# A hybrid decoder layer: weight tiles of the MLP's chunk loop begin at other places, one transpose goes to another bank

## The chip, the core and the metric

The kernel runs on one NeuronCore of a Trainium2 chip. Its engines are TensorE (PE, matrix products into PSUM banks), VectorE (DVE), ScalarE (ACT), GpSimd (POOL) and SyncE (SP, which here only issues transfers). Each has its own queue of instructions and works through it in order; they wait for each other by semaphores. The metric is the device time of one execution in microseconds (us), lower is better.

## The reference

One decoder layer on 256 tokens of width 2048, in float32: a normalised input goes through one wide projection, half of it through sliding-window attention and half through a gated linear recurrence, both through an output projection, and the result is added to the input. Then comes the MLP, which is the part that matters here:

```python
h = rmsnorm(x, mlp_pre_gain[layer])
u = jax.nn.relu(jnp.einsum('bsd,df->bsf', h, w_up[layer]))
y = jnp.einsum('bsf,fd->bsd', u * u, w_down[layer])
x = x + rmsnorm(y, mlp_post_gain[layer])
```

`w_up` is 2048 x 8192 and `w_down` is 8192 x 2048.

## The kernel before

**Split weights.** Every weight tile (128 x 4 x 512 values, 1 MB) is loaded as float32, then split in two: ACT casts it to a rounded high tile `whi` (line 90), DVE subtracts that from the original and leaves the low tile `wlo` (line 91). PE multiplies high by high, high by low and low by high, so a product needs its high tile first and its low tile one matmul later.

**Chunk loop.** The MLP's inner width of 8192 is cut into 8 chunks of 1024. Chunk 0 is computed ahead of the loop with another set of tiles. From chunk 1 on, the up projection is done by Strassen's scheme: a chunk's weights are four quarters named X, P, Q (the lower right one) and R, with X loaded or added up several times (`X+P`, `X+Q` and so on, line 871, on DVE), and seven block products m1 to m7 in place of eight. In between stand the down projections of the chunk before (`d` tiles, lines 111 to 113, into bank `sc`). The loop is a list of segments; each uses one weight tile for 12 products (`up_seg`, line 867) or 24 (`down_seg`). For chunk 1 the list begins with the two halves of m1, the second half of chunk 0's first down column, the two halves of m5, then down, m6, down, m7.

**Order.** From line 657 on for PE and line 715 on for ACT, DVE and SP the order is that of the code (`manual_schedule`). For each segment k the loop at the end writes: the additions of segment k on DVE; the split of segment k + 2 (`prepare(k + 2)`: cast on ACT, subtraction on DVE); ACT's other work and the transposes ("turns") of segment k; its products; its loads. So a cast that waits holds up everything behind it on ACT.

**Rings.** Tiles of one tag share a ring of slots. A new tile takes a slot when the tile before in it is done with, and its first writer waits for that tile's last readers. At the loop's start the old pool of weight tiles (four slots for `whi`, four for `wlo`, three for raw tiles) is closed and the new one (`wpool_c`) is laid over the same memory, with two slots each for X, d, P and Q and three each for `whi` and `wlo`. What the first tiles of the new pool wait for is thus decided by which old tile lay there. Of the old tiles the last to be read is the pair `w00`, the first down tile of chunk 0, whose 24 products (`down_half(0, 0, 0, ...)`) are the last on PE before the loop. Before those come four blocks of up products with the old pairs 4, 5, 6 and 7, in this order.

In the built program of before, the first cast of the loop (X, segment 0) goes into the slot of the high tile of `w00`, the first Q tile into that of old high tile 5, the second Q tile into that of the low tile of `w00`, and the low tiles into the slots of old low tiles 7, 5 and 6. A tile named `unused` is asked for ahead of the first cast and never written.

**Turns.** A turn transposes a 128 x 512 tile on PE into a PSUM bank (four transposes), then ACT and DVE split it. Two turns bring sums of the activations (`turn_sum`, line 637, into banks `tr` and `o`, read by ACT line 639 and DVE line 640). Two more bring the second half of chunk 0's activations (`turn_u`, transposes line 669, square line 671 and cast 673 on ACT, subtraction 674 on DVE): the first into the third `sc` bank, the second into `tr`, which it shares with the first `turn_sum`. The turns' results `uT` are read by the first down segment of the loop.

Of the kernel before, what the change touches and what calls it, by code (L numbers as in the profile page):

```python
# [8 lines left out]
F32 = mybir.dt.float32  # L9
F32R = mybir.dt.float32r  # L10
# [5 lines left out]
P = 128  # L16
# [13 lines left out]
def tile_hybrid_layer(  # L30
# [17 lines left out]
    nc = tc.nc  # L48
# [13 lines left out]
    wp = [pool_w.__enter__()]  # L62
# [18 lines left out]
    def split_weight(src, raw=None, pieces=1, bufs=4, between=None):  # L81
        raw = load_raw(src) if raw is None else raw
        hi = wp[0].tile(list(raw.shape), F32R, tag="whi", name=nm("whi"), bufs=bufs)
        if between:
            between()
        lo = wp[0].tile(list(raw.shape), F32R, tag="wlo", name=nm("wlo"), bufs=bufs)
        n = raw.shape[1] // pieces
        for i in range(pieces):
            k = slice(i * n, (i + 1) * n)
            nc.scalar.copy(out=hi[:, k], in_=raw[:, k])  # L90
            nc.vector.tensor_tensor(out=lo[:, k], in0=raw[:, k], in1=hi[:, k].bitcast(F32), op=ALU.subtract)  # L91
        return hi, lo
# [573 lines left out]
    def turn_u(uT, cb, tb, u, tag, bufs):  # L666
        tp = bank(tag, bufs)
        for i in range(4):
            nc.tensor.transpose(tp[:, i * P:(i + 1) * P], u[:, i * P:(i + 1) * P], ident)
        u2 = upool.tile([P, 4, P], F32, tag="u2", name=nm("u2"), bufs=2)  # L670
        nc.scalar.activation(out=u2, in_=tp.rearrange("p (a t) -> p a t", a=4), func=AF.Square)
        hi, lo = (uT[cb][:, :, i, tb * P:(tb + 1) * P] for i in range(2))
        nc.scalar.copy(out=hi, in_=u2)
        nc.vector.tensor_tensor(out=lo, in0=u2, in1=hi.bitcast(F32), op=ALU.subtract)
# [120 lines left out]
    def half(tb, h):  # L795
        return hn[tb][:, h * 1024:(h + 1) * 1024]
# [4 lines left out]
    def turn_sum(src, c, tag="sc", bufs=3):  # L801
        t = sums[src[0]]
        turn_act(src[1][:, c * 512:(c + 1) * 512], *(t(slice(4 * c, 4 * c + 4), i) for i in range(2)), tag, bufs)
# [52 lines left out]
    def raw_tile(tag, wv, kt0, c0):  # L856
        t = wp[0].tile([P, 4, 512], F32, tag=tag, name=nm(tag), bufs=2)
        nc.sync.dma_start(out=t, in_=wv[:, kt0:kt0 + 4, c0:c0 + 512])
        return t
# [63 lines left out]
    def relu_first(tb):  # L923
        prev[1, tb] = new_u()
        relu(prev[1, tb], ps[tb])
# [15 lines left out]
    def load_up(name, ch, h):  # L941
        kt0 = (8 if name in "QR" else 0) + 4 * h
        raws[name, ch, h] = raw_tile("P" if name == "R" else name, w_up_v, kt0, ch * 1024 + (512 if name in "PQ" else 0))
# [44 lines left out]
    def t(ch, cb, tb, dst, tag="sc", bufs=3):  # L988
        return lambda: turn_u(uTs[dst], cb, tb, us[ch][cb, tb], tag, bufs)

    def period(ch, m1_next):
        d = ch - 1
# [7 lines left out]
        if ch == 1:  # L1000
            q = [None, m1_first[0], m1_first[1], dn[0][1], m5[0], m5[1], dn[1][0], m6[0], m6[1], dn[1][1],
                 m7[0], m7[1], dn[2][0], m3[0], m3[1], dn[2][1], m4[0], m4[1], m2[0], m2[1],
                 m1_next[0], dn[3][0], m1_next[1], dn[3][1]]
        else:
            q = [m5[0], m5[1], dn[0][0], m6[0], m6[1], dn[0][1], m7[0], m7[1], dn[1][0], m3[0], m3[1], dn[1][1],
                 m4[0], m4[1], dn[2][0], m2[0], m2[1], dn[2][1], m1_next[0], dn[3][0], m1_next[1], dn[3][1]]
# [34 lines left out]
        if ch == 1:  # L1041
            q[1].turns += [lambda c=c: turn_sum(("s4", half(0, 0)), c, ("tr", "o")[c], 1) for c in range(2)]
            q[1].turns.append(t(d, 1, 0, d))
            q[2].turns.append(t(d, 1, 1, d, "tr", 1))
            loads = [(1, "d", d, 1, 1), (4, "d", d, 2, 0), (7, "d", d, 2, 1),
                     (8, "R", ch, 0), (9, "R", ch, 1), (10, "d", d, 3, 0), (11, "Q", nx, 0), (12, "Q", nx, 1),
                     (13, "d", d, 3, 1), (14, "X", nx, 0), (15, "X", nx, 1), (16, "P", nx, 0), (17, "P", nx, 1),
                     (19, "d", ch, 0, 0), (21, "d", ch, 0, 1)]
        else:
            q[0].turns += [t(d, 0, 0, d), t(d, 0, 1, d)]  # L1050
            q[3].turns.append(t(d, 1, 0, d))
            q[4].turns.append(t(d, 1, 1, d))
            loads = [(0, "d", d, 1, 0), (3, "d", d, 1, 1), (5, "R", ch, 0), (6, "R", ch, 1), (6, "d", d, 2, 0),
                     (9, "d", d, 2, 1), (12, "d", d, 3, 0), (15, "d", d, 3, 1),
                     (17, "d", ch, 0, 0), (19, "d", ch, 0, 1)]
            if nx < NCH:
                loads += [(8, "Q", nx, 0), (9, "Q", nx, 1), (11, "X", nx, 0), (12, "X", nx, 1), (14, "P", nx, 0),
                          (15, "P", nx, 1)]
# [14 lines left out]
    for ch in range(1, NCH):  # L1073
        m1 = first_products(ch + 1) if ch < NCH - 1 else [None, None]
        part, q = period(ch, m1)
        if ch == 1:
            q[3].adds.append(late_y)
        if ch < NCH - 1:
            part[-1].loads.append(lambda ch=ch: uTs.update({ch: new_uT()}))
        else:  # L1080
            last = NCH - 1
            q[14].turns.append(lambda: uTs.update({last: new_uT("mu2", "mu3")}))
            q[14].turns.append(t(last, 1, 1, last, "pj"))
            q[15].turns.append(t(last, 1, 0, last, "pj"))
            q[16].turns.append(t(last, 0, 1, last, "pj"))
            q[19].turns.append(t(last, 0, 0, last, "pj"))

            def load_residual():
                tail["x2"] = []
                for tb in range(2):  # L1090
                    xr = wp[0].tile([P, D], F32, tag="X", name=nm("x2"), bufs=2)
                    nc.sync.dma_start(out=xr, in_=x2_dram[tb])
                    tail["x2"].append(xr)

            def load_gain():
                tail["g"] = wp[0].tile([P, D], F32, tag="Q", name="gmlp", bufs=2)
                nc.sync.dma_start(out=tail["g"], in_=mlp_post.broadcast_to([P, D]))

            q[21].loads.append(load_gain)
        segs += part  # L1100
# [17 lines left out]
    def prepare(k, between=None):  # L1118
        segs[k].w = split_weight(None, segs[k].raw(), bufs=3, between=between)

    wp[0].tile([P, 4, 512], F32R, tag="whi", name="unused", bufs=3)
    prepare(0, lambda: [load_up("Q", 1, h) for h in range(2)])
    relu_first(0)
    prepare(1)
    relu_first(1)
# [46 lines left out]
```

## Time and profile before

| | us |
|---|---|
| three runs | 1112.05, 1112.89, 1113.70; median 1112.89 |
| profiled execution, its time | 1112.53 |
| its span | 1110.8 |
| PE busy | 1084.3 (98%) |
| DVE busy | 816.2 (73%) |
| ACT busy | 622.8 (56%) |
| POOL busy | 37.6 (3%) |

The profile's times count from the span's start; 1.7 us of the execution lie outside the span. The chunk loop begins at 466 us. A matmul's end is modelled, and matmuls overlap in the pipeline, so on PE the starts are the times to go by: a 128 x 512 product starts every 0.227 us when nothing holds it. In an idle time "<-" names what ended it.

### The profile page before, as it was taken

What the parts mean: (1) busy time and instruction counts of PE and PEld (TensorE: products, weight loads), DVE (VectorE), ACT (ScalarE), POOL (GpSimd) and SP (SyncE); (2) the same over time, 40 slices, a digit from 0 to 9 for tenths busy, and PEclk for the clock granted to TensorE, in tenths of its full rate; (3) what the DMA queues carried; (4) which work ended last, traced back from release to release, by engine and by line L of the source; (5) the groups of instructions that cost most, each with busy time, mean ns of one, the idle gap of its engine ahead of it and who ended that gap; (6) DMA issues with size and microseconds to landing.
All of it is one profiled execution on the core that took longest, in us unless ns stands there. A gap on an engine that the chain in (4) does not pass through costs nothing.

```text
span 1110.8 us, 14084 instructions
## 1 busy us (share of the span) xinstructions
PE 1084.3 (98%) x5708; PEld 924.8 (83%) x5708; DVE 816.2 (73%) x751; ACT 622.8 (56%) x719; POOL 37.6 (3%) x62
## 2 busy tenths in 40 slices
PE   8999989999999999989999999999999999999996
PEld 7999889998988877768788888888888888888885
DVE  6755666665654557597897897897897897897565
ACT  6554565545453454456665565565565565575542
POOL 2100000000000000000000000000000000000000
PEclk9999989999999999989999999999999999999998
DMA  8743424444458736829659559559559559556672
GB/s 271 246 160 121 151 77 153 152 152 152 152 190 298 232 133 218 293 81 279 246 161 332 192 159 331 191 158 332 191 157 333 190 158 333 190 156 186 236 256 76
DMA packets 132931, 224.30 MB, mean 202 GB/s; under 512 B 4169, under 2 KB 49794, under 8 KB 131842
## 3 DMA queue, kind: packets, MB, share of 16 engines
q1 hardware_dynamic: 125474, 208.72, 54.7%
q0 software_dynamic: 7392, 14.68, 7.5%
q8 instruction: 45, 0.74, 0.3%
q14 instruction: 20, 0.16, 0.0%
HBM read 219.19 MB, written 4.19 MB: 201 GB/s over the span
## 4 chain that ended last, share of the span: by engine, by line
PE 90%; DVE 3%; ACT 2%; issue 1%; DMA 1%; POOL 0%; DVEq 0%; POOLq 0%; ACTq 0%
PE pj L867 22%; PE pj L112 10%; PE pj L113 10%; PE pj L111 10%; PE sc L113 8%; PE sc L111 8%; PE sc L112 8%; PE o L112 1%; PE tr L113 1%; PE o L113 1%; PE tr L112 1%; PE tr L111 1%; PE o L111 1%; PE pj L730 1%; DVE wlo L91 1%
## 5 line engine op out<-in xcount | busy, mean ns | idle before, releaser
L91 DVE TENSOR_TENSOR wlo<-raw,whi 128x2048 fp32r<-128x2048 f32 (+2 forms) x77 | 145.6, 1900 | 75.2 <-ACT whi L90 75.1
L91 DVE TENSOR_TENSOR wlo<-d,whi 128x2048 fp32r<-128x2048 f32 x59 | 135.0, 2288 | 71.8 <-ACT whi L90 71.7
L90 ACT CAST whi<-d 128x2048 fp32r<-128x2048 f32 x59 | 112.9, 1913 | 123.6 <-PE sc L113 89.0
L90 ACT CAST whi<-raw 128x2048 fp32r<-128x2048 f32 (+2 forms) x77 | 121.7, 1595 | 75.4 <-PE pj L113 32.3
L90 ACT CAST whi<-X 128x2048 fp32r<-128x2048 f32 x56 | 107.2, 1915 | 80.1 <-PE sc L113 21.1
L111 PE MATMUL sc<-whi,uT 128*128 128x512 f32 x384 | 149.5, 389 | 0.0
L113 PE MATMUL sc<-whi,uT 128*128 128x512 f32 x384 | 149.4, 389 | 0.0
L112 PE MATMUL sc<-wlo,uT 128*128 128x512 f32 x384 | 149.4, 389 | 0.0
L867 PE MATMUL pj<-whi,hT 128*128 128x512 f32 x448 | 145.5, 394 | 0.0
L91 DVE TENSOR_TENSOR wlo<-X,whi 128x2048 fp32r<-128x2048 f32 x56 | 127.9, 2285 | 14.8 <-ACT whi L90 14.8
L111 PE MATMUL pj<-hT,whi 128*128 128x256 f32 x384 | 110.3, 287 | 0.9 <-ACT whi L90 0.6
L113 PE MATMUL pj<-hT,wlo 128*128 128x256 f32 x384 | 110.3, 287 | 0.9 <-DVE wlo L91 0.8
L112 PE MATMUL pj<-hT,whi 128*128 128x256 f32 x384 | 111.0, 289 | 0.0
L867 PE MATMUL pj<-whi,a 128*128 128x512 f32 x336 | 109.8, 395 | 0.0
L867 PEld LDWEIGHTS pj<-whi,hT 128*128 128x128 f32 x448 | 85.2, 190 | 17.7
L867 PE MATMUL pj<-wlo,hT 128*128 128x512 f32 x224 | 88.1, 393 | 0.9 <-DVE wlo L91 0.9
L91 DVE TENSOR_TENSOR wlo<-P,whi 128x2048 fp32r<-128x2048 f32 x32 | 73.3, 2290 | 15.9 <-ACT whi L90 15.9
L112 PEld LDWEIGHTS sc<-wlo,uT 128*128 128x128 f32 x384 | 72.1, 188 | 15.0
L113 PEld LDWEIGHTS sc<-whi,uT 128*128 128x128 f32 x384 | 72.1, 188 | 15.0
L111 PEld LDWEIGHTS sc<-whi,uT 128*128 128x128 f32 x384 | 72.0, 188 | 14.9
L111 PEld LDWEIGHTS pj<-hT,whi 128*128 128x128 f32 x384 | 73.9, 192 | 1.8 <-ACT whi L90 0.8
L113 PEld LDWEIGHTS pj<-hT,wlo 128*128 128x128 f32 x384 | 73.9, 192 | 1.6 <-DVE wlo L91 1.5
(277 smaller groups left out, 2028.6 us busy)
## 6 DMA issues: line engine op xcount, KB each, us to landing
d<-in_w_down_dram SPq DMA_DIRECT2D x59, 1024.0 KB, 5.1
P<-in_w_up_dram SPq DMA_DIRECT2D x28, 1024.0 KB, 6.1
raw<-in_w_in_dram SPq DMA_DIRECT2D x24, 1024.0 KB, 5.2
raw<-in_w_in_dram SPq DMA_DIRECT2D x35, 512.0 KB, 4.6
raw<-in_w_out_dram SPq DMA_DIRECT2D x16, 1024.0 KB, 5.2
X<-in_w_up_dram SPq DMA_DIRECT2D x14, 1024.0 KB, 6.0
Q<-in_w_up_dram SPq DMA_DIRECT2D x14, 1024.0 KB, 8.9
X<-in_w_up_dram POOLq DMA_DIRECT2D x14, 1024.0 KB, 10.8
```

The costliest lines, as they stand in the source:

```text
L90: nc.scalar.copy(out=hi[:, k], in_=raw[:, k])
L91: nc.vector.tensor_tensor(out=lo[:, k], in0=raw[:, k], in1=hi[:, k].bitcast(F32), op=ALU.subtract)
L111: nc.tensor.matmul(o, lhsT=ah, rhs=bh, start=first, stop=False)
L112: nc.tensor.matmul(o, lhsT=ah, rhs=bl, start=False, stop=False)
L113: nc.tensor.matmul(o, lhsT=al, rhs=bh, start=False, stop=last)
L730: nc.tensor.matmul(ps[tb], lhsT=a, rhs=b, start=kt == 0 and kind == "hh", stop=kt == NKT - 1 and kind == "hl")
L867: nc.tensor.matmul(o, lhsT=a, rhs=b, start=fresh and kt == 0 and i == 0, stop=kt == 7 and i == 2, skip_group_check=not fresh)
```

## The change

Three edits. The transposes of the second `turn_u` go into bank `sc` instead of `tr`. In place of the tile `unused`, a tile `skip0` is taken from the ring of `whi` and GpSimd writes two columns of it. The two loads of Q come after the first split in the code, where they stood between the first high tile and the first low tile.

```diff
             q[1].turns.append(t(d, 1, 0, d))
-            q[2].turns.append(t(d, 1, 1, d, "tr", 1))
+            q[2].turns.append(t(d, 1, 1, d))
...
-    wp[0].tile([P, 4, 512], F32R, tag="whi", name="unused", bufs=3)
-    prepare(0, lambda: [load_up("Q", 1, h) for h in range(2)])
+    skip = wp[0].tile([P, 4, 512], F32, tag="whi", name="skip0", bufs=3)
+    nc.gpsimd.memset(skip[:, 0, 0:2], 0.0)
+    prepare(0)
+    for h in range(2):
+        load_up("Q", 1, h)
     relu_first(0)
```

In the built program of after, `skip0` takes the slot of the high tile of `w00`. The first cast goes into the slot of old high tile 6, the second into that of old high tile 7, the third (the `d` tile) into that of `skip0`. The low tiles take the slots of old high tile 5, old low tile 7 and the low tile of `w00`. The Q tiles take those of old low tiles 6 and 5. All later tiles of the loop follow in these rings. The number and kind of instructions is the same on every engine but POOL, which has the memset more.

On ACT, at the loop's start, before (the number behind a name tells one buffer from another; `whi_4373`, `whi_4383` and `whi_4390` are the high tiles of segments 0, 1 and 2; the names in brackets are the engines or transfer queues that the row waits for):

```order
L639 CAST a_4135<-sc_4306 128x4x128 [waits PE_49]
L90 CAST whi_4373<-X_4360 128x2048 [waits DMAHW4_49,DVE_49,PE_49]
L664 ACTIVATE u_4381<-pj_4153 128x512
L90 CAST whi_4383<-X_4362 128x2048 [waits DMAHW5_49]
L664 ACTIVATE u_4387<-pj_4154 128x512
L90 CAST whi_4390<-d_4364 128x2048 [waits DMAHW6_49]
L639 CAST hT_3352<-tr_4394 128x4x128 [waits PE_49]
L639 CAST hT_3353<-o_4401 128x4x128 [waits PE_49]
L671 ACTIVATE u_4413<-sc_4408 128x512 [waits PE_49]
L673 CAST uT_3962<-u_4413 128x4x128 [waits Activation_49]
```

and after:

```order
L639 CAST a_4135<-sc_4306 128x4x128 [waits PE_49]
L90 CAST whi_4374<-X_4360 128x2048 [waits DMAHW4_49,DVE_49]
L664 ACTIVATE u_4382<-pj_4153 128x512
L90 CAST whi_4384<-X_4362 128x2048 [waits DMAHW5_49,DVE_49,PE_49]
L664 ACTIVATE u_4388<-pj_4154 128x512
L90 CAST whi_4391<-d_4364 128x2048 [waits DMAHW6_49,Pool_49]
L639 CAST hT_3352<-tr_4395 128x4x128 [waits PE_49]
L639 CAST hT_3353<-o_4402 128x4x128 [waits PE_49]
L671 ACTIVATE u_4414<-sc_4409 128x512 [waits PE_49]
L673 CAST uT_3962<-u_4414 128x4x128 [waits Activation_49]
```

Nothing changes place; the waits move. The first cast loses its wait for PE (the last product with `w00`). The second gets one, for the last product of the block with old pair 7. The third waits for POOL, whose memset itself waits for the last product with `w00`.

On PE, at the second `turn_u`, between the two halves of m1, before and then after:

```order
L867 MATMUL pj_4417<-wlo_4378,hT_3352 128x512
L867 MATMUL pj_4417<-whi_4373,hT_3352 128x512
L669 MATMUL tr_4437<-ident,u_4387 128x128 [waits DVE_49]
L669 MATMUL tr_4437<-ident,u_4387 128x128 x3
L867 MATMUL pj_4417<-whi_4383,hT_3353 128x512
L867 MATMUL pj_4417<-wlo_4384,hT_3353 128x512
```

```order
L867 MATMUL pj_4418<-wlo_4375,hT_3352 128x512
L867 MATMUL pj_4418<-whi_4374,hT_3352 128x512
L669 MATMUL sc_4438<-ident,u_4388 128x128 [waits Activation_49]
L669 MATMUL sc_4438<-ident,u_4388 128x128 x3
L867 MATMUL pj_4418<-whi_4384,hT_3353 128x512
L867 MATMUL pj_4418<-wlo_4385,hT_3353 128x512 [waits DVE_49]
```

Before, the turn waits for DVE's last reading of `tr` (the subtraction of the first `turn_sum`); after, for ACT's square of the first `turn_u`, which is the last reading of that `sc` bank.

## Rows read from the trace of the kernel before

**Rows 1.** The waits of PE, the first three from 436 to 512 us, the last from 484 us to the end: who waited for whom, us in total, times, the longest.

```profile
PE tr L669 <- DVE hT L640: 4.5, 1, 4.5
PE sc L669 <- ACT u L664: 1.6, 1, 1.6
PE pj L867 <- DVE wlo L91: 0.9, 1, 0.9
...
PE o L112 <- DVE wlo L91: 0.6, 1, 0.6
```

**Rows 2.** PE in order of time through the loop's start (start us, us, line, operation, tiles; in brackets the idle time before).

```profile
466.02 0.39 PE L113 MATMUL sc<-whi,uT 128*128 128x512 f32 x1
466.25 0.60 PE L637 MATMUL tr<-ident,hn 128*128 128x128 f32 x4
...
468.89 0.65 PE L669 MATMUL sc<-ident,u 128*128 128x128 f32 x4 [1.61 <-ACT u L664]
469.31 0.47 PE L867 MATMUL pj<-whi,hT 128*128 128x512 f32 x1
470.72 0.50 PE L867 MATMUL pj<-wlo,hT 128*128 128x512 f32 x1 [0.94 <-DVE wlo L91]
...
478.01 1.11 PE L669 MATMUL tr<-ident,u 128*128 128x128 f32 x4 [4.49 <-DVE hT L640]
...
483.75 0.40 PE L111 MATMUL sc<-whi,uT 128*128 128x512 f32 x1
...
505.52 0.39 PE L111 MATMUL sc<-whi,uT 128*128 128x512 f32 x1
```

**Rows 3.** ACT in order of time, the same stretch.

```profile
458.23 0.59 ACT L639 CAST a<-sc 128x512 fp32r<-128x512 f32 x1 [2.61 <-PE sc L637]
466.44 1.90 ACT L90 CAST whi<-X 128x2048 fp32r<-128x2048 f32 x1 [7.63 <-PE sc L113]
...
471.01 1.91 ACT L90 CAST whi<-d 128x2048 fp32r<-128x2048 f32 x1
472.81 0.59 ACT L639 CAST hT<-tr 128x512 fp32r<-128x512 f32 x1
...
473.76 0.63 ACT L671 ACTIVATE u<-sc 128x512 f32<-128x512 f32 x1
474.42 0.62 ACT L673 CAST uT<-u 128x512 fp32r<-128x512 f32 x1
```

**Rows 4.** DVE in order of time, the same stretch and on to the second down segment after it.

```profile
468.38 4.58 DVE L91 TENSOR_TENSOR wlo<-X,whi 128x2048 fp32r<-128x2048 f32 x2 [8.84 <-ACT whi L90]
472.87 2.28 DVE L871 TENSOR_TENSOR X<-X,P 128x2048 f32<-128x2048 f32 x1
475.07 2.28 DVE L91 TENSOR_TENSOR wlo<-d,whi 128x2048 fp32r<-128x2048 f32 x1
477.27 0.68 DVE L640 TENSOR_TENSOR hT<-tr,hT 128x512 fp32r<-128x512 f32 x1
...
478.47 0.68 DVE L674 TENSOR_TENSOR uT<-u,uT 128x512 fp32r<-128x512 f32 x1
...
483.48 0.68 DVE L674 TENSOR_TENSOR uT<-u,uT 128x512 fp32r<-128x512 f32 x1
...
502.95 2.28 DVE L91 TENSOR_TENSOR wlo<-d,whi 128x2048 fp32r<-128x2048 f32 x1
```

**Rows 5.** Stretches of 2 us (us, then busy time and instructions of PE, PEld, DVE, ACT and POOL, the granted clock, the share of the DMA engines, GB/s).

```profile
474.00:476.00 2.00, 0.00 (x0) 0.00 (x0) 2.00 (x2) 1.77 (x3) 0.00 (x0) 1.00 0.00 0
...
480.00:482.00 2.00, 2.00 (x6) 1.52 (x6) 2.00 (x2) 0.41 (x1) 0.00 (x0) 0.50 0.98 379
...
484.00:486.00 2.00, 2.00 (x10) 1.68 (x9) 2.00 (x2) 2.00 (x2) 0.00 (x0) 1.00 0.00 0
```

**Rows 6.** Transfers: SP's issues of the second P and of the two Q in order of time (start us, us), and under them the time from issue to landing (the last figure of a row, us) of that P and of the first Q, each asked for by a window around its issue.

```profile
456.99 0.50 SPq L858 DMA_DIRECT2D P<-in_w_up_dram  x1
457.54 0.51 SPq L858 DMA_DIRECT2D Q<-in_w_up_dram  x1
466.21 0.37 SPq L858 DMA_DIRECT2D Q<-in_w_up_dram  x1
...
P<-in_w_up_dram SPq DMA_DIRECT2D x1, 1024.0 KB, 8.8
Q<-in_w_up_dram SPq DMA_DIRECT2D x1, 1024.0 KB, 10.8
```

**Rows 7.** POOL by line and form (x count, busy us, mean ns of one), and one of its operations in order of time with the DVE operation that released it.

```profile
L152 POOL MEMSET mhalf<- 128x8 f32 x1 | 0.1, 105 | 0.0
...
397.50 0.15 DVE L599 TENSOR_TENSOR rf<-pss,ppart 128x1 f32<-128x1 f32 x1
397.73 0.55 POOL L600 TENSOR_TENSOR rf<-rf,mhalf 128x1 f32<-128x1 f32 x1 [63.17 <-DVE rf L599]
```

**Rows 8.** Stretches of the loop, columns as in rows 5.

```profile
460.00:490.00 30.00, 22.95 (x97) 18.33 (x96) 21.59 (x13) 14.67 (x15) 0.00 (x0) 0.89 0.44 154
490.00:530.00 40.00, 40.00 (x178) 33.11 (x177) 31.69 (x17) 26.02 (x20) 2.82 (x2) 1.00 0.86 247
```

**Rows 9.** The page's groups of low-tile subtractions by the tile they read.

```profile
L91 DVE TENSOR_TENSOR wlo<-d,whi 128x2048 fp32r<-128x2048 f32 x59 | 135.0, 2288 | 71.8 <-ACT whi L90 71.7
L91 DVE TENSOR_TENSOR wlo<-P,whi 128x2048 fp32r<-128x2048 f32 x32 | 73.3, 2290 | 15.9 <-ACT whi L90 15.9
```

## The prediction

> **What bounds the kernel now.** I read the waits of PE first. From 484 us to the end PE waits for anyone hardly at all: the longest wait is 0.6 us [rows 1]. In the loop's first 20 us it waits three times, 1.6, 0.9 and 4.5 us [rows 1]. So whatever is won or lost at the loop's start should reach the end unchanged, and the change touches that place. Next, PE in order of time [rows 2]. The last product with `w00` starts at 466.02 and ends at 466.41. The two `turn_sum` follow from 466.25; then PE stands until 468.89 (first `turn_u`), 470.72 (first low tile of m1) and 478.01 (second `turn_u`). Then ACT and DVE [rows 3, 4]. ACT has its input for the first cast of the loop and is idle from 458.8, but begins at 466.44, released by PE: its slot held `w00`. Everything else hangs on that cast: the relu that the first turn needs stands behind it on ACT, DVE idles 8.84 us for it, and from 468.38 DVE has an unbroken queue. The subtraction after the first `turn_sum` comes up at 477.27, and for it the second turn waits, since both use bank `tr`. [...]
>
> **What the start costs before.** PE's starts give it whole. From 483.75 to 505.52 stand 96 products (segments of 24, 24, 24 and 24), 0.2268 us each [rows 2]. The second down segment that begins at 505.52 ends at 505.52 + 24 x 0.2268 = 510.96. From 466.25 to there lie 44.71 us. The work in it is 144 products x 0.2268 = 32.66 and four turns at 0.42 (468.89 to 469.31 [rows 2]) = 1.68, together 34.34. Lost: 10.4 us, of which 7.0 are the three waits and most of the rest the half clock (478.01 to 483.75 is 5.74 us for a turn and 12 products, 3.14 at full clock).
>
> **The change, part by part.** I set up the same queues with the new waits; durations are those of rows 2 to 4.
>
> *First two casts.* The first waits for nothing late: old pair 6 was last read two blocks before `w00`. It starts when ACT is free, 458.8. Behind it the relu (0.5 us more of ACT), and the second cast from about 461.05, when the block before `w00` has ended on PE (24 products before 466.25, plus the 0.16 by which an end lies behind the next start), to 462.95. DVE subtracts the two from 460.7 and 463.0 and is done at 465.2. Removed: all three waits as they stand.
>
> *Third cast and the memset.* The `d` tile's cast now waits for POOL, POOL for PE at 466.41. The trace shows no such handover; it is bounded by a wake of 0.08 us after 63 us of rest (DVE ends at 397.65, POOL starts at 397.73) and a small memset of 0.105 us [rows 7]. From below: 466.44, as if there were no memset; from above: a memset that cannot begin before DVE's running addition ends, 467.5, hence a cast from 467.7. I take 466.65, by the nearest rows. Behind this cast stand on ACT the casts of both `turn_sum`, the square and the cast of the first `turn_u`: at 1.80 + 0.48 + 0.48 after it (471.01 to 473.76 in rows 3) the square starts, 469.4, and ends at 470.0. PE reaches the second turn at 466.25 + 3 x 0.42 + 2.72 = 470.25, so its new wait costs nothing; it would cost what the handover takes beyond 0.2 us.
>
> [...]
>
> *DVE from there.* X + P begins at 465.25 if P has landed. The second P landed at 456.99 + 8.8 = 465.8 [rows 6] and the first was issued before it, so the addition starts by 465.8 and ends by 468.0. The subtraction of `d` then begins at 468.6, behind its cast (466.65 + 1.91). From here DVE's queue is unbroken. It runs at 2.20 us a large instruction and 0.60 a small one (472.87, 475.07, 477.27; 477.27 to 478.47 holds two small ones [rows 4]). First small ones: 470.8, 471.4, 472.0 (lo of the first turn, ready 472.7). Then X + P second half, the low tile of m5, 472.6 to 477.0; the lo of the second turn at 477.0, ready 477.7. X + Q, low, X + Q reach 484.2. Then the low tiles of the next down segment (484.2 to 486.5), of m6 and P + Q in between (four instructions), and of the second down segment, 495.2 to 497.5.
>
> *PE.* First half of m1 467.5 to 470.25, turn, second half 470.7 to 473.4. The first down segment starts 473.4; its first 12 products find all they need (472.7). The second 12 need the second turn's lo at the third product, 476.6, and get it at 477.7: 1.15 us lost, end 480.0. m5 runs to 485.4. The next down segment needs its low tile at 485.7, gets it at 486.5: 0.85 lost, end 491.7. m6 ends 497.2; the second down segment loses 0.1 and ends at 502.75. The clock should stay up: 1.6 and 0.9 us of waiting in before still left it at 1.00 in 474 to 476 [rows 1, 5].
>
> *Q and the bank.* The second Q, issued at 466.21 because it waited for `w00`, goes out right behind the first, at 458.1 [rows 6]. X + Q is not due before 477.6, so this alone is worth nothing, and it can cost: four transfers are then under way. The bank takes away the 4.49 us wait on the `turn_sum`'s subtraction; without it the second turn would wait until 471.4, about 1 us, and DVE would still set the pace.
>
> **Sum.** 510.96 - 502.75 = 8.2 us: 10.4 lost before, 2.1 lost now. What follows keeps its distances, for its casts, subtractions and loads are released by PE and DVE. From the profiled execution, 1112.53 - 8.2 = 1104.3. The median of the runs shown is 0.36 above that execution, so from it 1104.7 would follow; I keep 1104.3.
>
> **Rivals.**
>
> *DVE's queue starts later (5 to 7.2 us won).* If the memset is held by the addition, everything from the `d` cast moves by 1.0: 7.2, 1105.3. If the four transfers share the engines evenly, P is late: the landings of P and Q lie 2.5 us apart (465.8 and 468.3 [rows 6]), a fourth load adds as much, so X + P begins by 468.3 and `d` is subtracted from 470.5, 1.9 later: 6.3 won, 1106.2. For it: DVE's queue decides everything after. Against: SP issues P first, and Q is far from due.
>
> *No new waits (9.2 to 10.4 won).* Without any, PE ends the second down segment at 466.25 + 34.34 = 500.6: 1102.2. That needs DVE 2.1 us earlier, which a free third cast alone doesn't give. A part of it is possible.
>
> *Given back (within 2 us of before, 1112).* A later stage is bound by transfers, and PE catches up with it. For it: the DMA engines are 0.86 busy from 490 to 530 [rows 8]. Against: they were at 0.44 in the 30 us before, and PE has no wait in that stretch; one transfer of 1 MB more or less overlapped doesn't fill 8 us.
>
> *Slower.* The tiles' new places make each subtraction longer for the whole loop. DVE is busy 31.69 of 40 us in the loop [rows 8], so it becomes the bound where its instructions take more than 40 / 31.69 = 1.26 times as long; at 1.30 the loop's 600 us grow by 3.2%, 19 us, and the kernel would take 1123. At 1.28 it breaks even with what the start wins. Against: subtractions of `d` and of P, which fall in different slots of the ring, both take 2.29 us [rows 9].
>
> **How the numbers follow.** Forecast (7.2 to 9.2 won, 1103.3 to 1105.3): 0.60. Later DVE queue: 0.17. More than 9.2: 0.10. Between 2.2 and 5: 0.02. Given back: 0.07. Slower: 0.04. What this kernel's runs can tell from no change is about 0.2%, 2.2 us; so faster 0.89, same 0.07, slower 0.04. The range 1102.2 to 1107.2 takes in all bounds of the DVE queue from both sides and holds 0.87.
>
> **What would show it.** After the change the first cast of X should stand at about 458.8, DVE's first subtraction at 460.7, the memset at 466.5 and the third cast within 0.3 us of it, the second turn right behind the first half of m1, and PE's clock at 1.00 throughout. Two waits of about 1 us on DVE should stand in the first two down segments, and the second of these end near 502.8. It is wrong if DVE's queue has a gap behind X + P, if the clock still falls, if P lands after 468, or if waits of PE turn up beyond 520 us.

## The result, and the profile after

The kernel after takes 1105.41 us (median; 1104.18 to 1105.61), the kernel before 1113.28 us on the same chip, with the runs shown above among its own. The ratio is 0.9931, interval 0.9919 to 0.9943: 7.9 us less, where 8.2 were forecast. The forecast time of 1104.3 was counted from the profiled execution of before, 1112.53; 8.2 below the 1113.28 measured here is 1105.1.

The profiled execution has a span of 1103.5 us, 7.3 less than before. Where these 7.3 us come from is read from PE's starts, in three pieces:

| us | before | after |
|---|---|---|
| span's start to the first `turn_sum` | 466.25 | 467.10 |
| from there to the end of the third down segment | 44.71 | 36.75 |
| from there to the span's end | 599.84 | 599.65 |

The middle piece, which I call the stretch from here on, is 7.96 shorter. The first piece differs by 0.85 with the same instructions in it, and over the ten profiles of this study it lies between 465.9 and 468.5; this is how executions differ, and the reason to compare the stretch rather than the spans. The last piece is the same to 0.2 us: nothing of the gain is given back.

A word on names. The loop's first three down segments begin on PE, in the kernel after, at 474.37, 486.40 and 498.27 us. The stretch ends where the third of them does; the prediction and the expectations call that one "the second down segment", because they mean the second one behind that at the loop's start. From here on they are the first, second and third.

PE in order of time at the loop's start (it answers to rows 2; columns as there), the two places where it waits, and the first product behind the third down segment:

```profile
467.10 0.60 PE L637 MATMUL tr<-ident,hn 128*128 128x128 f32 x4
467.53 0.60 PE L637 MATMUL o<-ident,hn 128*128 128x128 f32 x4
467.97 0.60 PE L669 MATMUL sc<-ident,u 128*128 128x128 f32 x4
...
471.18 0.60 PE L669 MATMUL sc<-ident,u 128*128 128x128 f32 x4
...
478.55 0.50 PE L113 MATMUL sc<-whi,uT 128*128 128x512 f32 x1 [0.85 <-DVE uT L674]
...
487.48 0.50 PE L112 MATMUL sc<-wlo,uT 128*128 128x512 f32 x1 [0.69 <-DVE wlo L91]
...
503.85 0.39 PE L867 MATMUL pj<-whi,a 128*128 128x512 f32 x1
```

The last row in the kernel before, which ends the 44.71:

```profile
510.96 0.39 PE L867 MATMUL pj<-whi,a 128*128 128x512 f32 x1
```

The three waits of [rows 1] are gone. The four turns and the first half of m1 follow each other without a gap; the second turn stands right behind the first half of m1, at 471.18. Two shorter waits on DVE have come in, in the first and the second down segment.

ACT, the same stretch (answers to rows 3):

```profile
459.10 0.59 ACT L639 CAST a<-sc 128x512 fp32r<-128x512 f32 x1 [2.62 <-PE sc L637]
459.58 1.91 ACT L90 CAST whi<-X 128x2048 fp32r<-128x2048 f32 x1
461.39 0.60 ACT L664 ACTIVATE u<-pj 128x512 f32<-128x512 f32 x1
461.88 1.92 ACT L90 CAST whi<-X 128x2048 fp32r<-128x2048 f32 x1
463.68 0.61 ACT L664 ACTIVATE u<-pj 128x512 f32<-128x512 f32 x1
467.46 1.92 ACT L90 CAST whi<-d 128x2048 fp32r<-128x2048 f32 x1 [3.16 <-POOL skip L1122]
```

The first two casts and both relus now lie beside the last products with `w00`, in the time in which ACT was idle before. The third cast is the one that waits now. What it waits for is on POOL:

```profile
467.32 0.10 POOL L1122 MEMSET skip<- 128x2 f32 x1 [50.02 <-PE sc L113]
```

The last product with `w00` ends 0.16 after the first `turn_sum` starts, at 467.26; the memset starts 0.06 later and the cast 0.04 after the memset. The handover by POOL costs 0.2 us in all. And DVE (answers to rows 4):

```profile
461.52 4.60 DVE L91 TENSOR_TENSOR wlo<-X,whi 128x2048 fp32r<-128x2048 f32 x2 [1.12 <-ACT whi L90]
466.04 2.28 DVE L871 TENSOR_TENSOR X<-X,P 128x2048 f32<-128x2048 f32 x1
469.40 2.29 DVE L91 TENSOR_TENSOR wlo<-d,whi 128x2048 fp32r<-128x2048 f32 x1 [1.08 <-ACT whi L90]
...
473.41 2.29 DVE L871 TENSOR_TENSOR X<-X,P 128x2048 f32<-128x2048 f32 x1
...
477.81 0.69 DVE L674 TENSOR_TENSOR uT<-u,uT 128x512 fp32r<-128x512 f32 x1
...
482.94 2.29 DVE L871 TENSOR_TENSOR X<-X,Q 128x2048 f32<-128x2048 f32 x1
485.14 2.28 DVE L91 TENSOR_TENSOR wlo<-d,whi 128x2048 fp32r<-128x2048 f32 x1
...
493.95 2.28 DVE L871 TENSOR_TENSOR P<-P,Q 128x2048 f32<-128x2048 f32 x1
496.16 2.28 DVE L91 TENSOR_TENSOR wlo<-d,whi 128x2048 fp32r<-128x2048 f32 x1
```

From 469.40 to 502.84 DVE works without a pause, and PE's two waits end where DVE's rows at 477.81 and 485.14 do. The clock, in the two stretches with those waits (columns as in rows 5):

```profile
477.00:479.00 2.00, 1.15 (x6) 0.65 (x5) 2.00 (x3) 1.18 (x2) 0.00 (x0) 1.00 0.00 0
486.00:488.00 2.00, 1.30 (x6) 0.80 (x5) 2.00 (x2) 1.36 (x1) 0.00 (x0) 1.00 0.00 0
```

It stays at 1.00. In before it was at 0.50 from 477 to 483; the first and the last us of these:

```profile
477.00:478.00 1.00, 0.00 (x0) 0.00 (x0) 1.00 (x3) 0.14 (x1) 0.00 (x0) 0.50 0.00 0
...
482.00:483.00 1.00, 1.00 (x4) 0.81 (x3) 1.00 (x1) 0.00 (x0) 0.00 (x0) 0.50 0.00 0
```

### The profile page after: what moved, and what is told of

The parts are those of the page before. It is cut to its first block, busy times and chain, and to the rows that moved or that the text cites. A ratio compares the mean times of both kernels' runs of the same rounds, so it can differ in the third digit from the quotient of the medians.

```text
span 1103.5 us, 14088 instructions
## 1 busy us (share of the span) xinstructions
PE 1083.7 (98%) x5708; PEld 925.0 (84%) x5708; DVE 816.1 (74%) x751; ACT 622.7 (56%) x719; POOL 38.6 (3%) x63
## 4 chain that ended last, share of the span: by engine, by line
PE 89%; DVE 4%; ACT 2%; issue 2%; DMA 2%; POOL 0%; SPq 0%; DVEq 0%; POOLq 0%; ACTq 0%
PE pj L867 22%; PE pj L112 10%; PE pj L111 10%; PE pj L113 10%; PE sc L112 8%; PE sc L113 8%; PE sc L111 8%; DVE wlo L91 2%; PE o L112 1%; PE tr L113 1%; PE o L113 1%; PE tr L112 1%; PE tr L111 1%; PE o L111 1%; PE pj L730 1%
```

## The experiments

All are compared by the stretch: 44.71 before, 36.75 after, and 34.34 if PE had nothing but its work. A stretch comes from one profile of a kernel; the one kernel that was profiled twice gave 43.72 and 43.73.

**One part alone.** Three kernels, each the kernel before with one edit of the change. The first:

```diff
-            q[2].turns.append(t(d, 1, 1, d, "tr", 1))
+            q[2].turns.append(t(d, 1, 1, d))
```

> Only the second turn_u goes to bank sc; rings as before. My theory: DVE's queue, which begins only when the cast behind w00 is done (468.4 in before), sets the pace, so the 4.5 us wait is cut into smaller waits on DVE (about 1.0, 1.1, 2.5 and 1.0 us) and little is won: the stretch from the first turn_sum on PE to the end of the second down segment goes from 44.7 (before) to about 43.2 us, the kernel 1 to 2 us below before. Rival (the bank's wait was itself the cost): the 4.5 us wait and the half clock behind it, 2.6 us, go: 37.6 us, 7 us below before.

Measured: ratio 0.9991 (0.9982 to 1.0001), a stretch of 468.53 to 512.25 = 43.7 us. Its waits of PE, from 440 to 515 us (us in total, times, longest us):

```profile
PE sc L113 <- DVE uT L674: 2.4, 2, 1.9
PE sc L669 <- ACT u L664: 1.6, 1, 1.6
PE pj L867 <- DVE wlo L91: 0.9, 1, 0.9
```

The 4.5 us wait is gone and 1.0 us of the stretch is won, less than the 1.5 expected; the medians, 1112.22 and 1112.94, differ by 0.7 us, which isn't clear of noise. The rival falls: the bank's wait was only the place where PE met DVE's lateness, and without it PE meets it in the first down segment. The waits are fewer than I had listed, and I put that down to the clock, which fell: slow products (from 473.60 to 474.88 one starts every 0.43 us, against 0.227 at 1.00) fill time in which PE would have waited. Two stretches of 1 us of this kernel (columns as in rows 5):

```profile
473.00:474.00 1.00, 1.00 (x2) 0.83 (x3) 1.00 (x1) 1.00 (x2) 0.00 (x0) 0.51 0.05 18
476.00:477.00 1.00, 1.00 (x5) 0.78 (x5) 1.00 (x1) 0.97 (x3) 0.00 (x0) 0.78 0.00 0
```

The second kernel takes the skipped tile alone, with the Q loads still between the first high and the first low tile:

```diff
-    wp[0].tile([P, 4, 512], F32R, tag="whi", name="unused", bufs=3)
+    skip = wp[0].tile([P, 4, 512], F32, tag="whi", name="skip0", bufs=3)
+    nc.gpsimd.memset(skip[:, 0, 0:2], 0.0)
```

> Only the skipped high tile; the Q loads between first high and first low tile, and the turn in bank tr, as before. My theory: the first cast no longer waits for w00, DVE starts 7 us earlier, and that is nearly the whole gain: the stretch from the first turn_sum to the end of the second down segment takes about 36.9 us (after: 36.75), the kernel 7.5 to 8.2 us below before; the second turn waits about 1.2 us for bank tr, which the later waits on DVE swallow. Rival (the bank is worth 4.5 us and more): 41 us or above, 3.5 us below before.

Measured: 1105.11 us, ratio 0.9934 (0.9919 to 0.9949), a stretch of 468.42 to 505.17 = 36.75 us, to the hundredth that of after. Its first `turn_sum` and the first product behind the third down segment, on PE:

```profile
468.42 0.60 PE L637 MATMUL tr<-ident,hn 128*128 128x128 f32 x4
...
505.17 0.39 PE L867 MATMUL pj<-whi,a 128*128 128x512 f32 x1
```

Its waits of PE, again from 440 to 515 us:

```profile
PE tr L669 <- DVE hT L640: 1.0, 1, 1.0
PE sc L112 <- DVE wlo L91: 0.6, 1, 0.6
```

The second turn does wait for its bank, 1.0 us. The wait in the first down segment, 0.85 us in after, is gone in exchange. One edit of the three holds the whole gain.

The third kernel changes the order of the Q loads alone:

```diff
-    prepare(0, lambda: [load_up("Q", 1, h) for h in range(2)])
+    prepare(0)
+    for h in range(2):
+        load_up("Q", 1, h)
```

> Only the order of the Q loads and the first low tile, so that Q lies on old low tiles and its second load doesn't wait for w00; no skipped tile, turn in bank tr. My theory: the first cast still waits for w00, X + Q isn't due for 10 us after Q has landed; nothing: 44.7 us for the stretch, within 1 us of before. Rival (the late second Q held DVE up): 2 us or more below before.

Measured: ratio 1.0003 (0.9994 to 1.0013), a stretch of 467.64 to 512.41 = 44.8 us, and the three waits of rows 1 unchanged, 4.5, 1.6 and 0.9 us. The order of Q alone wins nothing.

**Skipped tile and bank, Q as before** (the two diffs above together).

> Skipped tile and bank, Q loads as before. My theory: as after, stretch 36.6 to 36.9 us. Rival (the order of Q matters beside the other two): 0.5 us or more above.

Measured in one execution: a stretch of 467.73 to 504.50 = 36.8 us. So the order of Q is worth nothing beside the other two edits either, and next to the kernel with the skipped tile alone, which differs from this one by the bank only, the bank is worth nothing.

**A longer memset.** If the third cast sets DVE's queue, and DVE's queue sets PE, a delay of that cast must come through.

```diff
-    nc.gpsimd.memset(skip[:, 0, 0:2], 0.0)
+    nc.gpsimd.memset(skip, 0.0)
```

> The kernel after, with the memset over the whole skipped tile (128x2048 in place of 128x2), about 1.9 us of GpSimd in place of 0.1. My theory: the third cast and with it the low tile of the first down segment set DVE's queue, so nearly all of the 1.8 us comes through: stretch 38.4 to 38.6 us, kernel 1.8 us above after (6 us below before). Rival (the third cast has slack): 36.75 us, as after.

Measured: 1106.64 us, ratio 0.9943 (0.9928 to 0.9958), a stretch of 465.89 to 504.36 = 38.5 us. The memset takes 1.71 us more, the stretch 1.72. (The 1.9 us expected is twice the 0.956 us that GpSimd's memset of 128x1024, `kz` in line 313, takes in before; the whole skipped tile took 1.81.) One row each of POOL, ACT and DVE in order of time of this kernel (columns as in the rows of PE above: start and duration in us, engine, line, operation and tiles, idle before and its releaser):

```profile
466.11 1.81 POOL L1122 MEMSET skip<- 128x2048 f32 x1 [50.07 <-PE sc L113]
467.95 1.91 ACT L90 CAST whi<-d 128x2048 fp32r<-128x2048 f32 x1 [4.89 <-POOL skip L1122]
469.89 2.29 DVE L91 TENSOR_TENSOR wlo<-d,whi 128x2048 fp32r<-128x2048 f32 x1 [2.80 <-ACT whi L90]
```

POOL, ACT and DVE hand the delay on one for one, and the rival (slack at the third cast) falls. By the medians, each against the runs of before taken with it, this kernel wins 6.3 us and the kernel after 7.9: 1.6 of the 1.7.

**DVE's order.** The rest of the loss, 36.75 - 34.34 = 2.4 us, should be DVE's queue. DVE idles 1.08 us before the `d` tile's subtraction, while X + P of the second half has its data (the second P landed at 457.86 + 8.8 = 466.7); and the second X + Q and the second P + Q (482.94 and 493.95 in the rows above) stand ahead of the low tiles of the second and the third down segment, though they are due only later.

```diff
-            plan = [(1, "X", "P", ch, 0), (2, "X", "P", ch, 1), (3, "X", "Q", ch, 0), (4, "X", "Q", ch, 1),
-                    (6, "P", "Q", ch, 0), (7, "P", "Q", ch, 1), (12, "X", "R", ch, 0), (14, "X", "R", ch, 1),
+            plan = [(1, "X", "P", ch, 0), (1, "X", "P", ch, 1), (3, "X", "Q", ch, 0), (5, "X", "Q", ch, 1),
+                    (6, "P", "Q", ch, 0), (8, "P", "Q", ch, 1), (12, "X", "R", ch, 0), (14, "X", "R", ch, 1),
```

> The kernel after, with three additions of chunk 1 at other places of DVE's queue: the second X + P into the 1.1 us in which DVE waits for the third cast, the second X + Q and the second P + Q behind the low tiles of the two down segments. Same work. My theory (what is left at the loop's start is DVE's order alone): PE's waits of 0.8 and 0.7 us go, the stretch takes 34.6 to 35.0 us (34.34 is its work; after 36.75), the kernel 1.7 to 2.2 us below after, 9.5 to 10 below before. Rival (transfers bound the stretch once DVE doesn't): a new wait of PE of 1 us or more, stretch 36 us or above.

Measured: 1102.47 us, ratio to before 0.9905 (0.9890 to 0.9920), a stretch of 467.17 to 501.70 = 34.5 us. From 440 to 515 us PE has no wait left, so transfers don't bound the stretch either. PE's rows at the two ends of the stretch:

```profile
467.17 0.60 PE L637 MATMUL tr<-ident,hn 128*128 128x128 f32 x4
...
501.70 0.39 PE L867 MATMUL pj<-whi,a 128*128 128x512 f32 x1
```

This kernel's rows of DVE in order of time show what has moved:

```profile
466.09 4.49 DVE L871 TENSOR_TENSOR X<-X,P 128x2048 f32<-128x2048 f32 x2
470.49 2.29 DVE L91 TENSOR_TENSOR wlo<-d,whi 128x2048 fp32r<-128x2048 f32 x1
...
476.69 0.69 DVE L674 TENSOR_TENSOR uT<-u,uT 128x512 fp32r<-128x512 f32 x1
...
482.08 2.29 DVE L91 TENSOR_TENSOR wlo<-d,whi 128x2048 fp32r<-128x2048 f32 x1 [0.30 <-ACT whi L90]
```

The `d` tile comes 1.1 us later than in after, the second turn's lo 1.1 earlier, the next down tile 3.1 earlier. This version beats both kernels: its four runs lie from 1101.70 to 1103.89, those of after from 1104.18 to 1105.61, and its stretch is 2.2 us shorter.

**The bank once more.** In the kernel with the skipped tile alone the bank cost nothing because DVE was late behind it. With DVE's order mended that should change.

> The same additions moved, on top of the skipped tile alone: the second turn in bank tr and Q as before. My theory: the bank was worth nothing only because DVE was late anyway; now the second turn waits for the turn_sum's subtraction behind the moved addition, about 2.2 us, and nothing behind it swallows that: stretch 36.6 to 37.1 us, about 2 us above the run with the bank changed. Rival (the bank never matters): the same stretch as that run, within 0.3 us.

Measured: 1106.23 us, ratio 0.9940 (0.9923 to 0.9956), a stretch of 466.28 to 504.68 = 38.4 us, 3.9 above the run with the bank changed. PE's rows at the two ends:

```profile
466.28 0.60 PE L637 MATMUL tr<-ident,hn 128*128 128x128 f32 x4
...
504.68 0.39 PE L867 MATMUL pj<-whi,a 128*128 128x512 f32 x1
```

The rival falls, but the stretch is 1.3 us above the range that I had given. The wait is the 2.1 us that I had worked out; what I hadn't counted is the clock, which fell behind it. First the wait, from this kernel's waits of PE from 440 to 515 us:

```profile
PE tr L669 <- DVE hT L640: 2.1, 1, 2.1
```

And the clock behind it, in one stretch of 2 us of the same kernel (columns as in rows 5), at 0.50:

```profile
474.00:476.00 2.00, 2.00 (x6) 1.54 (x5) 2.00 (x2) 0.57 (x1) 0.00 (x0) 0.50 1.05 396
```

The two kernels also differ in the order of Q, which was worth nothing in both comparisons above; with the additions moved it wasn't tried alone, but the wait names the bank, and the clock falls right behind it. So the bank is worth 3.9 us, 2.1 of waiting and 1.8 behind it, but only where DVE is in time; in the change itself it is worth nothing that shows.

**The clock of the first kernel again.**

> The bank alone once more, for TensorE's clock: in the first look it fell at 473 us, behind the waits of 1.6 and 0.95 us that before passes at full clock. If that hangs on the order of these instructions, it falls at the same place again, and the stretch takes 43.7 us; if it varies from run to run, the clock falls elsewhere or not at all, and the stretch differs by 1 us or more.

Measured in one execution: a stretch of 467.99 to 511.72 = 43.7 us. The clock fell at the same place, from 472.8, in the first half of m1, and again, at 486.5, behind the wait in the first down segment.

## Why the prediction was right

*The cause.* Right: the first cast of the loop stood behind `w00`, and the skipped tile alone, which gives it another slot, wins everything.

*The first two casts.* With 0.85 taken off for the later start, the first cast stands at 458.7 (458.8 forecast) and DVE's first subtraction at 460.7 (460.7).

*The handover.* The cast behind POOL starts at 466.6, as taken (466.65). The bound from above, a memset that waits for DVE's addition, was an assumption of mine, and the 1.0 us of the first rival rests on it; no run shows such a wait. DVE's X + P runs from 466.04 to 468.32, and the memset starts in the middle of it, at 467.32, and takes 0.10 us. X + P takes 2.28 us there as in before. With the longer memset it is the same: X + P runs from 464.81 and takes 2.29 us, and the memset starts beside it at 466.11.

*P's landing.* X + P begins as soon as DVE is free, at 466.04, though all four transfers had been issued by 459.8. Less the 0.85 that is 465.2, where I had allowed until 465.8 for P. The second P lands 8.8 us after its issue in both kernels, the first Q 11.0 us (10.8 in before, where the second Q went out 8 us later), so the fourth transfer held up those two by no more than 0.2 us, and the rival of a later DVE queue has no ground. One of the signs of being wrong did turn up by its letter: DVE has a gap behind X + P, 1.08 us. My own working has one of 0.6 there (468.0 to 468.6), and the rest is X + P ending earlier; the subtraction of `d` begins at 468.55 once the 0.85 are taken off, as forecast (468.6), so the sign was badly put and the forecast of the queue holds.

*DVE and PE from there.* By PE's starts the third down segment ends at 503.00 after the 0.85 are taken off, where 502.75 was forecast (the last part of the prediction says "the second of these" for it); m5 begins at 480.1 (480.0), m6 at 492.0 (491.7). I had 2.1 us of waits left; the stretch holds 2.4 above its work, of which the profile calls 1.5 waiting. Most of the rest lies at the restarts: the starts around 478.55 lie 1.23 and 0.34 apart where the rhythm is 0.227, so 1.1 us are lost there against 0.85 called waiting.

*Q and the bank.* Q worth nothing: right, by its own run and beside the other two edits. The bank I put at nothing for the time, since DVE sets the pace; right in the change, shown by the equal stretches of the skipped tile with the bank and without it.

*The rivals.* Given back: no, the last piece of the table is the same. Slower for the whole loop by the tiles' new places: no, by the same row (its price was a little off: 1.30 x 31.69 / 40 is 1.030, so 18 us and not 19). No new waits: not in the change; it took another order on DVE to reach 34.5 us.

*What was wrong in the reasons.* I argued that the clock would stay up because waits of 1.6 and 0.9 us had left it at 1.00 in before. The kernel with the bank alone has the same two waits, and there the clock fell right behind them, in both of its profiles. The conclusion held for the change, whose two waits are shorter and 8 us apart, but that row didn't bear it: on the clock the prediction was lucky.

## What to carry to other kernels

When a new pool is laid over an old one, look at which old tile lies under the first tile of each ring: here the first writer inherited the wait for that tile's last reader, and what was queued behind it on its engine waited too (first cast and relu at 466.44 and 468.25 over the high tile of `w00`, at 459.58 and 461.39 over old high tile 6). A wait that a profile puts at 4.5 us on a bank may be no more than the place where an engine meets another's lateness: taking it away alone won 1.0 us, and it was worth 3.9 once the late engine had been mended. Where the engine that is late is busy without a pause, its order is the next thing to look at; here work that wasn't due yet stood ahead of work that was, and moving it won another 2.2 us.

## What the runs showed that was not expected

The clock. The same instructions with the same two waits of 1.6 and 0.9 us at the loop's start were followed by full clock (1.00) in before and in the kernel with the order of Q alone (it fell only in the 4.5 us of idle later, at 476.6 and 478.1), and by half clock (0.50) from 473.0 and 472.8 in the two profiles of the kernel with the bank alone. On PE the kernels don't differ up to that point. A wait of 2.1 us (second turn in bank `tr`, moved additions) was followed by half clock, a wait of 1.3 us in the kernel with the longer memset by full clock. What decides between them in this range stays open; no run here tells it. What it can cost is plain: 1.8 us in the last comparison, 3.9 in all where the wait alone was 2.1.
